# Decoder block on one core: longer first weight pieces and idle products in the opening, compression woven by step length, and the first norm's vectors loaded during the gate

## The chip, the cores and the metric

The kernel runs on one core of a Trainium2 chip. The metric is the device time of one execution in microseconds (us). TensorE is called PE here, VectorE DVE, ScalarE ACT, GpSimd POOL and SyncE SP, as in the profile.

## What is computed

One decoder block for 256 tokens of width 2048, all in float32. Cut to what matters:

```python
proj = x @ w_in
bg, cg, hx, q, k_c, v_c, k_s, v_s, k_w, v_w, ng, ma, mb = _split_in(proj)
y_a = (bg * _causal_dwconv(cg * hx, conv_w)) @ w_conv_out
o_nsa = _nsa(q, k_c, v_c, k_s, v_s, k_w, v_w, sigmoid(ng), pe_k, w1_k, w2_k, pe_v, w1_v, w2_v, rel_bias)
mixed = sigmoid(ma) * y_a + sigmoid(mb) * (o_nsa @ w_attn_out)
x = _layer_norm(DN_ALPHA * x + mixed @ w_mix_out, ln1_g, ln1_b)
h = square(relu(x @ w_mlp_up)) @ w_mlp_down
ple = (p @ w_ple) * sigmoid(x @ w_ple_gate)
x = _layer_norm(DN_ALPHA * x + h + ple, ln2_g, ln2_b)

def _compress(k, pe, w1, w2):      # used by _nsa for keys and for values
    blocks = k[:, idx] + pe        # 15 overlapping windows of 32 tokens, 4 heads
    return gelu(blocks.reshape(..., 32 * 128) @ w1) @ w2
```

## The kernel before

Every weight is read from HBM once, in chunks, by DMAs that SP issues (`load_raw`, L74, four `raw` buffers of 512 KB). A chunk is split into two float32r parts: ACT copies it to the high part `whi` (L82, four buffers), and DVE subtracts that from the chunk to give the low part `wlo` (L84, three buffers). Activations are split in the same way (`split`, L68 on ACT and L69 on DVE). A product is then the sum of three: high by high, high by low and low by high.

`wstat` keeps a weight tile in PE and streams the tokens: for each of 16 k-tiles (128 rows of the weight) and each tile of 128 columns, one 512-column product with `whi` (L100, both parts of the activation) and one 256-column product with `wlo` (L106). It works on 256 weight columns, so on two of the four `mm` buffers of PSUM, and its evacuation (here `add_to`, L185 on ACT and L186 on DVE) frees them. `xstat` keeps the tokens in PE and streams the weights (L127, L128, L131). Both are generators that yield after each chunk.

The opening (L208 to L251) loads x in eight pieces of two k-tiles (L211), turns each with four PE transposes (L179) into a `tp` buffer and splits it into X. The first `wstat`, on the first half of C_KC (256 columns), takes its weights in chunks of two k-tiles (256 KB) and calls `x_ahead`, which loads and turns the next piece of x. Then come a few small things (vectors, a table product `pr` L244, its copy `rv` L246, a store to DRAM `rd` L247 on POOL's queue, from which the first `bias` is read back on ACT's queue, L395, into DVE's copies `cb`, L399 and L400), and the other half of C_KC and the two halves of C_VC in chunks of four k-tiles (512 KB).

The next stage weaves two streams. The main one projects four halves of C_KS and C_KW (`wstat`), C_VS (`xstat` of 512 columns) and C_VW twice (`xstat` of 280 columns). The side one runs `compress` for keys and then for values (L257 to L327): PE turns the position embedding `pn` (L263) to `peT`, DVE adds it to the 32-token windows (L271, four times), ACT and DVE split the sum into `blk` (L68, L69), and PE multiplies `blk` by eight chunks of w1 into `ph` (L281, L282). `weave` gives the side stream 24 turns spread evenly over the 40 steps of the main one, each step counted alike.

Much later, ln1's factor and offset are loaded in broadcast form into `gb` on ACT's queue (L594, L595) behind the mix projection. The first norm, the per-layer embedding, the gate (L653 to L665) and then the MLP follow. The second norm's vectors `gb2` are loaded by L670 and L671.

The order on each engine comes from the tile framework's scheduler, which works from its own estimate of costs; `tc.issue_after(ins)` forces what is written inside it to be issued behind `ins`. Each engine then runs its list in that order and waits on semaphores. A step that waits holds up all that stands behind it on its engine.

Of the kernel before, what the change touches and what calls it, by code (L numbers as in the profile page):

```python
# [45 lines left out]
def block_kernel(ctx: ExitStack, tc: tile.TileContext, x, p, w_in, conv_w, cmp_pe_k, cmp_w1_k, cmp_w2_k,  # L46
# [19 lines left out]

    def split(src, hi, lo):
        nc.scalar.activation(hi, src, AF.Copy)  # L68
        return nc.vector.tensor_sub(lo, src, f32(hi)).ins  # L69

# [6 lines left out]
    def wchunk(src, nk, n, behind=None):  # L77

        raw = load_raw(src, nk, n)
        hi = wp.tile([P, nk, n], F32R, tag="whi", name="whi", bufs=4)  # L80
        lo = wp.tile([P, nk, n], F32R, tag="wlo", name="wlo", bufs=3)
        nc.scalar.activation(hi, raw, AF.Copy)  # L82
        with tc.issue_after(behind) if behind is not None else nullcontext():
            nc.vector.tensor_sub(lo, raw, f32(hi))  # L84
        return hi, lo

    def wstat(src, c0, mov, evac, r0=0, nk=4, ahead=None):


        ps = [ps_mm.tile([P, 2, T], F32, tag="mm", name="mm") for _ in range(2)]  # L90
        for k0 in range(0, KT, nk):
            hi, lo = wchunk(src[r0 + k0 * P:r0 + (k0 + nk) * P, c0:c0 + 256], nk, 256)
            for kk in range(nk):
                kt = k0 + kk
                if ahead is not None:
                    ahead(kt)

                def high():
                    for f in range(2):
                        nc.tensor.matmul(ps[f].rearrange("p a t -> p (a t)"), hi[:, kk, f * P:(f + 1) * P],  # L100
                                         mov[:, kt].rearrange("p a t -> p (a t)"), start=(kt == 0),
                                         stop=(kt == KT - 1), skip_group_check=True)

                def low():
                    for f in range(2):
                        nc.tensor.matmul(ps[f][:, 1, :], lo[:, kk, f * P:(f + 1) * P], mov[:, kt, 0, :],  # L106
                                         start=False, stop=False, skip_group_check=True)
# [4 lines left out]
        for f in range(2):  # L112
# [35 lines left out]
    def weave(main, n_main, side, n_side):  # L148

        done = 0  # L150
        for i, _ in enumerate(main):
            while done * n_main < (i + 1) * n_side:
                next(side, None)
                done += 1
        run(side)
# [16 lines left out]
    def transposed(nat, kt, behind=None):  # L172
# [3 lines left out]
        with tc.issue_after(behind) if behind is not None else nullcontext():  # L176
# [31 lines left out]
    with tc.tile_pool(name="front", bufs=1) as fp:  # L208
        xnat = big.tile([P, NT, D], F32, tag="B", name="xnat")
        def x_load(kt):  # L210
            nc.sync.dma_start(xnat[:, :, kt * P:(kt + 2) * P],  # L211
                              x[:, kt * P:(kt + 2) * P].rearrange("(t p) d -> p t d", p=P))
# [36 lines left out]
        run(wstat(w_in, C_KC + 256, X, add_to(craw[:, 0, 2:4])))  # L249
# [96 lines left out]
        weave(chain(*proj), 40, chain(compress(0, cmp_pe_k, cmp_w1_k, cmp_w2_k),  # L346
# [308 lines left out]

    for j in range(4):
        cs = slice(j * 512, (j + 1) * 512)

        def ev_gate(t, ps):
            sg = post.tile([P, 512], F32, tag="sg", name="sg")  # L660
            nc.scalar.activation(sg, ps, AF.Sigmoid)
# [3 lines left out]
                  behind=(lambda k2: x1_ts[k2]) if j == 0 else None))  # L665

# [126 lines left out]
```

## Time and profile before

| | |
|---|---|
| median of 3 runs | 1856.15 us (1854.9 to 1856.57) |
| the profiled execution | 1856.03 us |
| its span, first to last instruction | 1854.1 us |
| PE busy | 1831.3 us, 99% of the span |
| DVE, ACT busy | 61%, 46% |
| bytes moved | 352.92 MB, 190 GB/s on average |

The profile shows one execution. Its span leaves out some 1.9 us around the first and the last instruction. PE is busy nearly throughout, so the order of its instructions and the few places where it stands idle decide the time. A time is a start in us from the beginning of the span unless said otherwise. Records of products overlap, since PE is pipelined; the chain of waits gives the share of each without the overlap.

### The profile page before, as it was taken

The numbers are of one execution on the slowest core, as the hardware profiler recorded it, in microseconds if no ns is written. First come the engines' busy times: TensorE is split into PE (matmuls) and PEld (weight loads), VectorE is DVE, ScalarE is ACT, GpSimd is POOL, SyncE is SP. The second block draws the span as 40 slices with busy tenths as digits, with TensorE's granted clock in tenths as the row PEclk, the third lists the DMA queues.
The fourth block names the chain that finished last, engine by engine and source line by source line (L and its number), as shares of the span: only waits on it lengthen the run. The fifth ranks groups of instructions, "written<-read, shape, count | busy, mean of one in ns | idle before, by whom it ended". The sixth has DMA issues, their size and how long they took to land.

```text
span 1854.1 us, 24809 instructions
## 1 busy us (share of the span) xinstructions
PE 1831.3 (99%) x9441; PEld 1556.9 (84%) x9441; DVE 1129.0 (61%) x1571; ACT 861.0 (46%) x1181; POOL 16.6 (1%) x25
## 2 busy tenths in 40 slices
PE   8999999999999999999999999999999999999997
PEld 7889888888888888888888788888888888888886
DVE  6676776768677444455555655775565566556664
ACT  5555554455455444444443544543444344434541
POOL 1000000000000000000000000000000000000001
PEclk9999999999999999999999999999999999999999
DMA  8768565555555766666665556655665566556671
GB/s 245 231 200 240 170 174 158 162 170 169 168 161 157 243 194 194 193 187 188 192 230 194 205 194 190 191 186 197 191 188 193 193 193 187 192 189 193 194 248 69
DMA packets 262296, 352.92 MB, mean 190 GB/s; under 512 B 11126, under 2 KB 175318, under 8 KB 261409
## 3 DMA queue, kind: packets, MB, share of 16 engines
q1 hardware_dynamic: 258560, 342.27, 59.8%
q10 hardware_dynamic: 3232, 8.65, 1.4%
q8 instruction: 74, 1.21, 0.3%
q0 software_dynamic: 384, 0.41, 0.1%
q14 instruction: 46, 0.37, 0.1%
HBM read 349.17 MB, written 2.12 MB: 189 GB/s over the span
## 4 chain that ended last, share of the span: by engine, by line
PE 97%; DMA 1%; DVE 1%; ACT 0%; issue 0%; SPq 0%; POOLq 0%; POOL 0%; ACTq 0%; DVEq 0%
PE mm L100 29%; PE mm L131 16%; PE mm L128 16%; PE mm L127 16%; PE mm L106 15%; PE mm L739 1%; PE pss L444 1%; PE po L481 1%; PE tp L466 1%; DMA raw<-in_cmp_w_v_dram 0%; DMA raw<-in_w_ple_gate_dram 0%; PE tp L179 0%; PE po L490 0%; PE po L485 0%; DVE wlo L84 0%; PE pq L407 0%
## 5 line engine op out<-in xcount | busy, mean ns | idle before, releaser
L84 DVE TENSOR_TENSOR wlo<-raw,whi 128x1024 fp32r<-128x1024 f32 (+2 forms) x648 | 778.6, 1205 | 592.6 <-PE mm L131 319.7
L82 ACT ACTIVATE whi<-raw 128x1024 fp32r<-128x1024 f32 (+2 forms) x648 | 676.8, 1046 | 753.9 <-PE mm L128 434.2
L100 PE MATMUL mm<-xT,whi 128*128 128x512 f32 x1280 | 402.7, 398 | 0.0
L100 PE MATMUL mm<-x,whi 128*128 128x512 f32 x1024 | 316.9, 395 | 0.0
L106 PEld LDWEIGHTS mm<-xT,wlo 128*128 128x128 f32 x1280 | 234.9, 189 | 52.2 <-issue 0.2
L106 PE MATMUL mm<-xT,wlo 128*128 128x256 f32 x1280 | 250.6, 280 | 0.0
L106 PEld LDWEIGHTS mm<-x,wlo 128*128 128x128 f32 x1024 | 187.9, 188 | 42.5
L100 PEld LDWEIGHTS mm<-xT,whi 128*128 128x128 f32 x1280 | 200.3, 189 | 4.6 <-issue 0.6
L106 PE MATMUL mm<-x,wlo 128*128 128x256 f32 x1024 | 196.7, 279 | 0.0
L128 PE MATMUL mm<-whi,h 128*128 128x512 f32 x480 | 186.8, 389 | 0.0
L127 PE MATMUL mm<-whi,h 128*128 128x512 f32 x480 | 186.8, 389 | 0.0
L100 PEld LDWEIGHTS mm<-x,whi 128*128 128x128 f32 x1024 | 158.5, 189 | 2.8
L131 PE MATMUL mm<-wlo,h 128*128 128x512 f32 x480 | 148.0, 390 | 0.4 <-DVE wlo L84 0.4
L127 PE MATMUL mm<-whi,xT 128*128 128x512 f32 (+1 forms) x352 | 130.6, 374 | 1.5 <-ACT whi L82 1.4
L128 PE MATMUL mm<-whi,xT 128*128 128x512 f32 (+1 forms) x352 | 130.0, 372 | 0.0
L131 PEld LDWEIGHTS mm<-wlo,h 128*128 128x128 f32 x480 | 90.0, 188 | 19.8 <-DVE wlo L84 1.2
L128 PEld LDWEIGHTS mm<-whi,h 128*128 128x128 f32 x480 | 90.1, 188 | 18.8
L127 PEld LDWEIGHTS mm<-whi,h 128*128 128x128 f32 x480 | 90.1, 188 | 18.7
L131 PE MATMUL mm<-wlo,xT 128*128 128x512 f32 (+1 forms) x352 | 102.8, 373 | 0.0
L127 PEld LDWEIGHTS mm<-whi,xT 128*128 128x128 f32 x352 | 66.1, 188 | 13.2 <-ACT whi L82 1.9
L128 PEld LDWEIGHTS mm<-whi,xT 128*128 128x128 f32 x352 | 66.1, 188 | 11.2
L131 PEld LDWEIGHTS mm<-wlo,xT 128*128 128x128 f32 x352 | 63.9, 188 | 11.2
(216 smaller groups left out, 1773.3 us busy)
## 6 DMA issues: line engine op xcount, KB each, us to landing
raw<-in_w_in_dram SPq DMA_DIRECT2D x228, 512.0 KB, 3.7
raw<-in_w_mlp_up_dram SPq DMA_DIRECT2D x128, 512.0 KB, 3.8
raw<-in_w_mlp_down_dram SPq DMA_DIRECT2D x128, 512.0 KB, 4.0
raw<-in_w_conv_out_dram SPq DMA_DIRECT2D x32, 512.0 KB, 4.1
raw<-in_w_attn_out_dram SPq DMA_DIRECT2D x32, 512.0 KB, 3.6
raw<-in_w_mix_out_dram SPq DMA_DIRECT2D x32, 512.0 KB, 3.9
raw<-in_w_ple_gate_dram SPq DMA_DIRECT2D x32, 512.0 KB, 3.6
raw<-in_w_in_dram SPq DMA_DIRECT2D x16, 280.0 KB, 3.4
```

The source lines that it names most:

```text
L82: nc.scalar.activation(hi, raw, AF.Copy)
L84: nc.vector.tensor_sub(lo, raw, f32(hi))
L100: nc.tensor.matmul(ps[f].rearrange("p a t -> p (a t)"), hi[:, kk, f * P:(f + 1) * P], mov[:, kt].rearrange("p a t -> p (a t)"), start=(kt ...
L106: nc.tensor.matmul(ps[f][:, 1, :], lo[:, kk, f * P:(f + 1) * P], mov[:, kt, 0, :], start=False, stop=False, skip_group_check=True)
L127: nc.tensor.matmul(ps[t], sta[:, kt, 0, ts], hi[:, kk, :], start=(kt == 0), stop=False)
L128: nc.tensor.matmul(ps[t], sta[:, kt, 1, ts], hi[:, kk, :], start=False, stop=False)
L131: last_mm[0] = nc.tensor.matmul(ps[t], sta[:, kt, 0, ts], lo[:, kk, :], start=False, stop=(kt == nkt - 1)).ins
L444: nc.tensor.matmul(ps, q[:, g, a, t * P:(t + 1) * P], kT[:, j, b, :, :w], start=(n == 0), stop=(n == 2))
L466: nc.tensor.transpose(tp[:, b, k, :], s[:, b, k * P:(k + 1) * P], ident)
L481: nc.tensor.matmul(po, vn[:, b, 0, a, vs], pT[:, c, b, 0:2], start=(n == 0 and b == 0), stop=False, skip_group_check=True)
L739: nc.tensor.matmul(ps, h[:, kt, a, ts], w[:, kt, :], start=(kt == 0 and n == 0), stop=(kt == KT - 1 and n == 2))
```

## The change

It does four things.

1. `wchunk` can put `whi` and `wlo` each behind a given instruction, and `wstat` takes the number of 128-column tiles, `nf`.
2. The opening: twelve products of a zeroed tile (128x64, float32, result unused) are put on PE ahead of the first transposes. All 512 columns of C_KC go through one `wstat` with `nf=4`, in chunks of two k-tiles that now hold 512 KB and with all four `mm` buffers; the run for its second half is gone. Pieces of x are loaded one step earlier. The transposes of a piece stand behind the last product written so far. `whi` of a chunk stands behind the high split of the same piece of x, `wlo` behind the low split.
3. `weave` takes a length for each main step: 4 for the 24 steps of 512 KB, 2 for the 16 of 280 columns. The side stream's 24 turns go by length.
4. The loads of ln1's factor and offset move from behind the mix projection to behind the sigmoids of the gate's first and second column block.

```diff
     def split(src, hi, lo):
-        nc.scalar.activation(hi, src, AF.Copy)
+        last_hi[0] = nc.scalar.activation(hi, src, AF.Copy).ins
         return nc.vector.tensor_sub(lo, src, f32(hi)).ins
...
     def wchunk(src, nk, n, behind=None):
...
-        nc.scalar.activation(hi, raw, AF.Copy)
-        with tc.issue_after(behind) if behind is not None else nullcontext():
+        low, high = behind if isinstance(behind, tuple) else (behind, None)
+        with after(high):
+            nc.scalar.activation(hi, raw, AF.Copy)
+        with after(low):
             nc.vector.tensor_sub(lo, raw, f32(hi))
...
-    def wstat(src, c0, mov, evac, r0=0, nk=4, ahead=None):
-        ps = [ps_mm.tile([P, 2, T], F32, tag="mm", name="mm") for _ in range(2)]
+    def wstat(src, c0, mov, evac, r0=0, nk=4, ahead=None, nf=2, behind=None):
+        ps = [ps_mm.tile([P, 2, T], F32, tag="mm", name="mm") for _ in range(nf)]
         for k0 in range(0, KT, nk):
-            hi, lo = wchunk(src[r0 + k0 * P:r0 + (k0 + nk) * P, c0:c0 + 256], nk, 256)
+            hi, lo = wchunk(src[r0 + k0 * P:r0 + (k0 + nk) * P, c0:c0 + nf * P], nk, nf * P,
+                            behind(k0 // nk) if behind is not None else None)
...
     def weave(main, n_main, side, n_side):
-        done = 0
-        for i, _ in enumerate(main):
-            while done * n_main < (i + 1) * n_side:
+        lengths = [1] * n_main if isinstance(n_main, int) else n_main
+        done, at, total = 0, 0, sum(lengths)
+        for step, _ in zip(lengths, main, strict=True):
+            at += step
+            while done * total < at * n_side:
                 next(side, None)
                 done += 1
-        run(side)
+        run(main, side)
...
+        x_split = []
         def x_turn(kt):
-            tp = transposed(xnat, kt)
-            split(tp, X[:, kt:kt + 2, 0, :], X[:, kt:kt + 2, 1, :])
+            tp = transposed(xnat, kt, last_mm[0])
+            low = split(tp, X[:, kt:kt + 2, 0, :], X[:, kt:kt + 2, 1, :])
+            x_split.append((low, last_hi[0]))
         def x_ahead(kt):
-            if kt % 2 == 0 and kt + 2 < KT:
-                x_load(kt + 2)
-                x_turn(kt + 2)
+            if kt == 0:
+                x_load(2)
+            if kt % 2 == 0 and kt + 4 < KT:
+                x_load(kt + 4)
+            if kt % 2 and kt + 1 < KT:
+                x_turn(kt + 1)
...
+        idle = fp.tile([P, P], F32, name="idle")
+        nc.vector.memset(idle, 0.0)
+        for _ in range(12):
+            pw = ps_po.tile([P, 64], F32, tag="po", name="pw")
+            last_mm[0] = nc.tensor.matmul(pw, idle, idle[:, :64], start=True, stop=True).ins
         x_turn(0)
-        run(wstat(w_in, C_KC, X, add_to(craw[:, 0, 0:2]), nk=2, ahead=x_ahead))
+        run(wstat(w_in, C_KC, X, add_to(craw[:, 0]), nk=2, ahead=x_ahead, nf=4,
+                  behind=lambda k: x_split[k]))
...
-        run(wstat(w_in, C_KC + 256, X, add_to(craw[:, 0, 2:4])))
...
-        weave(chain(*proj), 40, chain(compress(0, cmp_pe_k, cmp_w1_k, cmp_w2_k),
+        weave(chain(*proj), [4] * 24 + [2] * 16, chain(compress(0, cmp_pe_k, cmp_w1_k, cmp_w2_k),
...
-    nc.scalar.dma_start(gb[:, 0, :], ln1_g.to_broadcast([P, D]))
-    nc.scalar.dma_start(gb[:, 1, :], ln1_b.to_broadcast([P, D]))
...
+        if j < 2:
+            with tc.issue_after(gated[-1]):
+                nc.scalar.dma_start(gb[:, j, :], (ln1_g, ln1_b)[j].to_broadcast([P, D]))
```

What the scheduler makes of it is seen in the order of the engines. PE in the opening, before (x4 are the transposes of one piece of x, `mm` the products):

```order
L179 MATMUL tp<-ident,xnat 128x128 x12
L100 MATMUL mm<-xT,whi 128x512 x2
L106 MATMUL mm<-xT,wlo 128x256 x2
L100 MATMUL mm<-xT,whi 128x512 x2
L106 MATMUL mm<-xT,wlo 128x256 x2
L100 MATMUL mm<-xT,whi 128x512 x2
L106 MATMUL mm<-xT,wlo 128x256 x2
```

and in the change, where old L179, L100 and L106 are L192, L109 and L116:

```order
L250 MATMUL pw<-idle 128x64 x12
L192 MATMUL tp<-ident,xnat 128x128 x4
L109 MATMUL mm<-xT,whi 128x512 x4
L116 MATMUL mm<-xT,wlo 128x256 x4
L192 MATMUL tp<-ident,xnat 128x128 x4
L109 MATMUL mm<-xT,whi 128x512 x4
L116 MATMUL mm<-xT,wlo 128x256 x4
L109 MATMUL mm<-xT,whi 128x512 x4
L116 MATMUL mm<-xT,wlo 128x256 x4
L192 MATMUL tp<-ident,xnat 128x128 x4
```

Three pieces of x were turned ahead of the first product; now one is, and each further one is turned behind the low products of the even k-tile of the chunk before it. ACT and DVE now alternate strictly: split of a piece of x, split of its weight chunk.

DVE around the end of C_KC, before (L186 evacuates `mm`, L271 adds `peT`, `O_88` holds the raw keys and values):

```order
L84 TENSOR_TENSOR wlo<-raw,whi 128x1024 x2
L186 TENSOR_TENSOR O_88<-O_88,mm 128x256
L265 COPY peT<-tp 128x32
L186 TENSOR_TENSOR O_88<-O_88,mm 128x256
L271 TENSOR_TENSOR O_88<-O_88,peT 128x32x15 x2
L84 TENSOR_TENSOR wlo<-raw,whi 128x1024
L399 COPY cb<-bias 128x4x7
L400 COPY cb<-bias 128x4x15
L84 TENSOR_TENSOR wlo<-raw,whi 128x1024 x3
```

and in the change (old L84, L186, L271, L399, L69 are L92, L199, L296, L424, L72):

```order
L72 TENSOR_TENSOR xT<-tp,xT 128x2x256
L92 TENSOR_TENSOR wlo<-raw,whi 128x1024
L340 MEMSET hx 128x512
L92 TENSOR_TENSOR wlo<-raw,whi 128x1024 x3
L199 TENSOR_TENSOR O_88<-O_88,mm 128x256 x4
L296 TENSOR_TENSOR O_88<-O_88,peT 128x32x15 x4
L424 COPY cb<-bias 128x4x7
L425 COPY cb<-bias 128x4x15
L72 TENSOR_TENSOR blk<-O_88,blk 128x32x60
L92 TENSOR_TENSOR wlo<-raw,whi 128x1024 x4
```

The first `wlo` row here is the last chunk of C_KC. The evacuation of all four buffers now stands behind the first three low parts of C_VC, and the fourth low part of C_VC behind the evacuation, the copies that wait for `bias`, and `blk`.

DVE at the second compression, before:

```order
L265 COPY peT<-tp 128x32
L271 TENSOR_TENSOR O_88<-O_88,peT 128x32x15 x4
L84 TENSOR_TENSOR wlo<-raw,whi 128x1024 x2
L69 TENSOR_TENSOR blk<-O_88,blk 128x32x60
L84 TENSOR_TENSOR wlo<-raw,whi 128x560
```

and in the change:

```order
L290 COPY peT<-tp 128x32
L335 TENSOR_TENSOR kc<-pk,kc 128x4x15
L296 TENSOR_TENSOR O_88<-O_88,peT 128x32x15 x4
L427 CAST kcp<-kc 128x2x4x16
L92 TENSOR_TENSOR wlo<-raw,whi 128x1024
L72 TENSOR_TENSOR blk<-O_88,blk 128x32x60
L92 TENSOR_TENSOR wlo<-raw,whi 128x1024 x8
```

On PE the transpose of `pn` and the first `ph` are now four and a half k-tiles of the 512-column `xstat` apart (a whole k-tile four times, then the high products of one more); before there were six whole k-tiles and the high products of a 280-column one.

## Rows read from the trace of the kernel before

**Rows 1.** The core's span and mean granted clock

```profile
core 0: 1854.1 us, clock 0.998
```

**Rows 2.** Timeline of PE in the opening: start, us, what [idle before <-releaser]

```profile
3.87 1.08 PE L179 MATMUL tp<-ident,xnat 128*128 128x128 f32 x4 [3.87 <-DMA xnat<-in_x_dram]
5.95 1.12 PE L179 MATMUL tp<-ident,xnat 128*128 128x128 f32 x4 [1.00 <-DMA xnat<-in_x_dram]
...
13.00 0.60 PE L179 MATMUL tp<-ident,xnat 128*128 128x128 f32 x4
```

**Rows 3.** Chain of waits, opening and C_VC: start us, us, what

```profile
8.75 0.85 PE mm L100 x2
...
12.46 0.47 PE mm L100 x2
...
35.84 0.93 PE mm L100 x4
...
46.54 0.47 PE mm L106 x4
...
57.70 0.47 PE mm L106 x4
```

**Rows 4.** Timeline of ACT in the opening, columns as in rows 2

```profile
5.42 0.63 ACT L82 ACTIVATE whi<-raw 128x512 fp32r<-128x512 f32 x1 [3.18 <-DMA raw<-in_w_in_dram]
5.96 0.58 ACT L68 ACTIVATE xT<-tp 128x512 fp32r<-128x512 f32 x1
...
13.63 0.60 ACT L68 ACTIVATE xT<-tp 128x512 fp32r<-128x512 f32 x1 [0.20 <-PE tp L179]
...
20.86 1.06 ACT L82 ACTIVATE whi<-raw 128x1024 fp32r<-128x1024 f32 x1 [0.45 <-PE mm L100]
21.84 0.48 ACT L246 ACTIVATE rv<-pr 16x384 f32<-16x384 f32 x1
...
26.89 0.40 ACTq L395 DMA_DIRECT2D bias<-rd  x1
```

**Rows 5.** Timeline of DVE in the opening

```profile
22.43 0.48 DVE L315 MEMSET hx<- 128x512 f32 x1
23.48 2.36 DVE L84 TENSOR_TENSOR wlo<-raw,whi 128x1024 fp32r<-128x1024 f32 x2 [0.57 <-issue]
25.76 0.41 DVE L186 TENSOR_TENSOR O<-O,mm 128x256 f32<-128x256 f32 x1
...
32.91 0.19 DVE L399 COPY cb<-bias 128x28 f32<-128x28 f32 x1 [3.34 <-DMA bias<-rd]
```

**Rows 6.** Timeline of PE around the first compression's end: a float32 product

```profile
123.46 0.55 PE L306 MATMUL pk<-g,w2s 128*128 128x60 f32 x4
123.82 0.48 PE L128 MATMUL mm<-whi,xT 128*128 128x512 f32 x1
```

**Rows 7.** Tile bias: all four reads, us to landing

```profile
DMA to landing us min/median/max: 3.4/4.6/6.0
```

**Rows 8.** Timeline of DVE at the second compression

```profile
126.62 3.75 DVE L271 TENSOR_TENSOR O<-O,peT 128x480 f32<-128x480 f32 x4
...
132.56 2.15 DVE L69 TENSOR_TENSOR blk<-O,blk 128x1920 fp32r<-128x1920 f32 x1
```

**Rows 9.** Timeline of PE at the second compression

```profile
125.16 0.24 PE L263 MATMUL tp<-ident,pn 32*128 32x32 f32 x1
...
134.85 0.35 PE L281 MATMUL ph<-whi,blk 128*120 128x256 f32 x1 [0.56 <-DVE blk L69]
```

**Rows 10.** Stretches: us, busy of PE, PEld, DVE, ACT, POOL, clock, DMA, GB/s

```profile
8.00:12.00 4.00, 4.00 (x15) 3.42 (x14) 2.48 (x5) 1.75 (x3) 0.00 (x0) 1.00 1.09 326
...
148.00:153.00 5.00, 3.64 (x29) 3.42 (x28) 1.97 (x2) 2.23 (x3) 0.00 (x0) 1.00 0.85 266
158.00:163.00 5.00, 4.87 (x38) 4.62 (x37) 3.70 (x6) 2.97 (x6) 0.00 (x0) 1.00 0.66 175
```

**Rows 11.** Stretches after ln1's loads and at the norm, same columns

```profile
945.00:955.00 10.00, 10.00 (x49) 8.29 (x48) 4.73 (x5) 3.59 (x5) 0.00 (x0) 1.00 0.98 374
...
1035.00:1045.00 10.00, 8.35 (x44) 6.54 (x43) 4.97 (x9) 5.59 (x9) 0.00 (x0) 1.00 0.70 273
1045.00:1055.00 10.00, 8.20 (x38) 6.27 (x38) 9.23 (x16) 6.94 (x12) 0.00 (x0) 1.00 0.31 109
```

**Rows 12.** Tile gb: the loads of the second norm's factor

```profile
L670 ACTq DMA_DIRECT2D gb<-in_ln_g_dram x1: 334/334/334, 1031.1 to 1031.1; - x1
```

More of the change, by code (lines that the diff above doesn't have):

```diff
@@ L65, in f32, with after @@
         return ap.bitcast(F32)
+    def after(ins):
+        return tc.issue_after(ins) if ins is not None else nullcontext()
     def split(src, hi, lo):
-        nc.scalar.activation(hi, src, AF.Copy)
+        last_hi[0] = nc.scalar.activation(hi, src, AF.Copy).ins
         return nc.vector.tensor_sub(lo, src, f32(hi)).ins
+    last_hi = [None]
     def load_raw(src, nk, n):
@@ L98, in high @@
                 def high():
[L99 to L102, printed above, removed]
+                    for f in range(nf):
+                        last_mm[0] = nc.tensor.matmul(
+                            ps[f].rearrange("p a t -> p (a t)"), hi[:, kk, f * P:(f + 1) * P],
+                            mov[:, kt].rearrange("p a t -> p (a t)"), start=(kt == 0), stop=(kt == KT - 1),
+                            skip_group_check=True).ins
                 def low():
-                    for f in range(2):
-                        nc.tensor.matmul(ps[f][:, 1, :], lo[:, kk, f * P:(f + 1) * P], mov[:, kt, 0, :],
-                                         start=False, stop=False, skip_group_check=True)
+                    for f in range(nf):
+                        last_mm[0] = nc.tensor.matmul(ps[f][:, 1, :], lo[:, kk, f * P:(f + 1) * P],
+                                                      mov[:, kt, 0, :], start=False, stop=False,
+                                                      skip_group_check=True).ins
                 for part in ((high, low) if kt < KT - 1 else (low, high)):
@@ L111, in wstat @@
             yield
-        for f in range(2):
+        for f in range(nf):
             evac(f, ps[f][:, 0, :], ps[f][:, 1, :])
@@ L175, in transposed @@
         tp = pool.tile([P, 2, T], F32, tag=tag, name="tp")
-        with tc.issue_after(behind) if behind is not None else nullcontext():
+        with after(behind):
             for k in range(2):
@@ L210, in x_load @@
         def x_load(kt):
-            nc.sync.dma_start(xnat[:, :, kt * P:(kt + 2) * P],
-                              x[:, kt * P:(kt + 2) * P].rearrange("(t p) d -> p t d", p=P))
+            return nc.sync.dma_start(xnat[:, :, kt * P:(kt + 2) * P],
+                                     x[:, kt * P:(kt + 2) * P].rearrange("(t p) d -> p t d", p=P)).ins
+        x_split = []
         def x_turn(kt):
-            tp = transposed(xnat, kt)
-            split(tp, X[:, kt:kt + 2, 0, :], X[:, kt:kt + 2, 1, :])
+            tp = transposed(xnat, kt, last_mm[0])
+            low = split(tp, X[:, kt:kt + 2, 0, :], X[:, kt:kt + 2, 1, :])
+            x_split.append((low, last_hi[0]))
         def x_ahead(kt):
-            if kt % 2 == 0 and kt + 2 < KT:
-                x_load(kt + 2)
-                x_turn(kt + 2)
+            if kt == 0:
[4 more added lines that the diff above has]
+                x_turn(kt + 1)
         warm = fp.tile([P, 1], F32, name="warm")
@@ L654, in x1_ahead @@
             x1_turn(kt + 6)
+    gated = []
     for j in range(4):
@@ L660, in ev_gate @@
             sg = post.tile([P, 512], F32, tag="sg", name="sg")
-            nc.scalar.activation(sg, ps, AF.Sigmoid)
+            gated.append(nc.scalar.activation(sg, ps, AF.Sigmoid).ins)
             nc.vector.tensor_mul(ple[:, t, cs], sg, ple[:, t, cs])
```

## Prediction

> **What bounds the kernel now.** I read the core's span first: 1854.1 us at a mean granted clock of 0.998 [rows 1]. The profiled execution took 1856.03 us, 0.12 below the median of 1856.15; the sum is made against 1856.03. PE is busy for 99% of the span, so there is almost nothing to win inside the long stages, and a part of the change counts only where PE starts late or stands idle. Three such places are touched.
>
> The first is the opening. PE waits for x until 3.87 and again at 5.95 [rows 2]. Its first products then run at 0.85 us for two of 512 columns, from 12.46 on at 0.47 [rows 3]. That is the ratio of TensorE's two levels, 1.2 and 2.4 GHz, though the column of the granted clock reads 1.00 in that stretch too [rows 10]. From there PE has no gap to the end of C_KC (35.84 + 0.93 = 36.8) and of C_VC (57.70 + 0.47 + 0.93 = 59.1) [rows 3]. One `wstat` of 64 products takes 57.70 - 46.54 = 11.16 us, a k-tile 0.70 [rows 3]. The second place is the second compression: PE waits 0.56 for `blk` [rows 9] and loses 5 - 3.64 = 1.36 and 5 - 4.87 = 0.13 us later in the weave [rows 10]. The third is the norm, where PE loses 1.65 and 1.80 us in two stretches, while the stretch behind ln1's loads is full [rows 11].
>
> A measurement of this kernel can tell about 0.2%, some 3.7 us, from no change.
>
> **The opening, chunk by chunk.** The products are the same in number. What changes is the chain that feeds them. In the new order the transposes of piece n stand behind the low products of the chunk before, and on ACT and DVE a chunk's split stands behind the split of its piece of x. So from the transposes of one piece to those of the next:
>
> - transposes to the start of the high split of x: 13.63 - 13.00 = 0.63 [rows 2, 4];
> - that split until ACT takes the next instruction: 5.96 - 5.42 = 0.54 between two of this size [rows 4];
> - `whi` of 1024 columns: 1.06 [rows 4];
> - `wlo`, half of 2.36: 1.18 [rows 5];
> - four low products: 0.47 [rows 3], and some 0.12 for three handovers at 0.03 to 0.05 (13.63 against 13.00 + 0.60 in the first item).
>
> That is 4.0 us. PE's own work per chunk is 0.44 for the transposes (an estimate, the 0.60 of [rows 2] less the overlap into the next product) and two k-tiles with 4 products of 0.235 and 0.47 of low ones: 3.25. PE stands idle for some 0.75 us in each of seven chunks. Before, it could work ahead, since three pieces had been turned before the first product, and a chunk's split was not tied to x.
>
> Start: x's first piece (256 KB) and the first chunk (now 512 KB) are 768 KB; before, 768 KB had landed at 5.95 [rows 2]. So `whi` ends at 7.0, `wlo` at 8.2, the second transposes start at about 8.8, those of the eighth piece, called E, at 8.8 + 6 x 4.0 = 32.8. C_KC ends at E + 4.0 + 0.47 + 0.93 = E + 5.4 = 38.2, against 36.8 before: +1.4. (Before, the slow products from 8.75 to 12.46 cost some 1.6 us: 3.7 us that would be 3.7 x 0.47 / 0.85 = 2.1. That loss is gone in this sum, if the first products now run fast; if not, it comes back once, in the first chunk.)
>
> **Idle products.** The nearest row is the two float32 products of 60 columns that take 123.82 - 123.46 = 0.36, so 0.18 each [rows 6]. Twelve of them from about 1.0 us end at 3.2, or at 5.3 at half the clock; the first transposes could not start before 3.87 anyway. The cost is 0, at most 1.4. I take 0, since PE is otherwise empty there.
>
> **The `mm` buffers.** C_KC now holds all four, so C_VC cannot start until DVE has added out the first two. DVE has before that: the last `wlo` (until E + 3.5), the memset `hx` 0.48, three `wlo` of C_VC at 1.18 and two adds of 0.41 [rows 5]: E + 8.4 for the second. PE's first product of the pair can go 0.23 earlier, so C_VC starts at E + 8.2. PE waits 2.8 us where it waited for nothing before.
>
> **The bias chain.** The fourth low part of C_VC now stands on DVE behind the copies that wait for `bias`, and behind `blk`. `rv` starts on ACT behind `whi` of the third chunk, at E + 2.2 + 3 x 1.06 = E + 5.4. From `rv` to the first copy it took 32.91 - 21.84 = 11.1 us (store, `bias` issue at 26.89, landing 6.0) [rows 4, 5]. So the copies come at E + 16.5, then some 0.3 for both, `blk` 2.15 [rows 8] and `wlo` 1.18: E + 20.1. PE gets there after 12 k-tiles and the high products of the thirteenth, E + 8.2 + 12 x 0.70 + 0.46 = E + 17.0. It waits 3.1 us. The four reads of `bias` land after 3.4 to 6.0 [rows 7]; at 3.4 the wait is 0.5. I take 6.0, the same transfer at the same place, and keep 0.5 as the bound.
>
> C_VC then ends at E + 8.2 + 2 x 11.16 + 3.1 = E + 33.6 = 66.4, against 59.1: **+7.3 us**. PE is full behind it, so nothing is made good.
>
> **The weave.** By length, the side stream's second start comes so that only four k-tiles of C_VS and four high products lie between the transpose of `pn` and `ph`: 0.2 + 0.4 for `pk` + 4 x 6 x 0.23 + 0.9 = 7.0 us. The windows' additions started 126.62 - 125.16 = 1.5 after that transpose [rows 8, 9]; with the copy of `kc` ahead of them 1.7. Then 3.75 for the additions, 1.8 for ACT's high half of `blk` (an estimate from its size, 1.06 for 1024 columns) and 2.15 for the low half: 9.4, and 0.1 to PE. PE waits 2.5 us in place of 0.56: +1.9. With 280-column steps and chunks of w1 spread by length, the 1.36 and 0.13 go: net **+0.5**, between -2.1 (no wait at all) and +2.
>
> **ln1's loads.** PE is full behind them [rows 11], so taking them away frees nothing. At the gate they stand on ACT's queue behind a sigmoid that has run, and nothing there waits for them until after the MLP's first products. 0, within 0.5 either way.
>
> **Sum:** 1856.03 + 7.3 + 0.5 = 1863.8 us. The case's own range is 1860 to 1867: 2.6 less if `bias` lands early, 2.6 less from the weave, 1 either way from seven chunks of 0.15, up to 1.4 more from late idle products, and not all of these at once.
>
> **Rivals.**
>
> *Faster: the chain does not bind.* If a chunk's step from transposes to transposes were not above PE's own 3.25 us, as it would be if the splits overlapped more than their rows show, the eighth transposes would start at 8.8 + 6 x 3.25 = 28.3 and C_KC end at 28.3 + 0.44 + 3 x 1.41 = 33.0, 3.8 earlier than before. With DVE no longer behind, the waits at C_VC fall away, and with 1.5 from the weave the time is about 1851. It decides at a step of 3.25 against my 4.0. For it: DVE and ACT have spare time in every chunk. Against: each link is in the order and has a row. 0.13.
>
> *No change: only the chunks cost.* If DVE takes the adds early enough and `bias` is not in the way, what is left is +1.4 from C_KC and +0.5: 1857.9. For it: the copies of `bias` waited 3.34 us before too [rows 5] with no loss on PE. Against: DVE runs its list in order, and three `wlo` stand ahead of the adds. 0.20.
>
> *The ln1 move clears the norm.* If the loads that crowd the norm were ln1's, the 3.45 us of [rows 11] would go: 1863.8 - 3.45 = 1860.4. But the loads there are the second norm's [rows 12], which stay. 0.05, still slower than before by over 0.2%.
>
> *Slower: the clock falls.* PE now has a gap in every chunk. If it ran at the lower of its two levels through the opening, the transposes would take 0.9 (the 1.08 of [rows 2], less the overlap) and the two k-tiles 4 x (0.85 + 0.43) = 5.1: 6.0 a chunk instead of 4.0, 14 us over seven chunks, so about 1878. For it: the products at 8.75 were slow after gaps of 1.00 and 0.57 us. Against: behind the gaps of the weave the clock stayed at 1.00 [rows 10]. 0.05. The Trainium skill, "TensorE: Matmul & The Clock Gate", section "A second HAM failure mode: psum-queue depth-cycling", says that short idle stretches between groups of matmuls can make the clock swing between its levels; no run of this kernel with a gap in each chunk is at hand, so by that rule alone it would be this rival.
>
> **How the numbers follow.** Forecast 0.57, faster 0.13, no change 0.20, the ln1 rival 0.05, the clock 0.05. The first and the last two are slower: 0.67. The range leaves out the clock's case and that of the faster rival, and reaches down over no change: 1855.5 to 1867.5. The time is that of the likeliest case.
>
> **What would show it.** Right: in the opening, idle of PE ahead of old L106 released by `wlo`, about seven times 0.4 and as much ahead of L100 released by `whi`; transposes 4.0 us apart; a wait of about 2.8 ahead of the first C_VC product released by the adds, with some 3 us lost in its first half to a late `wlo` behind the `bias` copies; some 2.5 before the second `ph`, and no loss in the 280-column steps; the stretches from 1035 on like those before, shifted. Wrong: transposes 3.3 us apart, or a C_VC without a gap at its start. A first product later than 8.4 would speak for late idle products.

## The result, and the profile after

The changed kernel takes 1867.26 us (median of 6 runs, 1866.53 to 1868.45) against 1856.36 for the kernel before in the same runs: 10.9 us slower, ratio 1.0061, 95% interval [1.0048, 1.0074]. The direction was right; the forecast of 1863.8 was 3.5 us short. The time lies just under the upper edge of the stated range (1867.5) and just above the 1860 to 1867 that the sum gave by itself.

The profiled execution took 1866.53 us, the fastest of the six. The page of the change:

```profile
span 1864.8 us, 24834 instructions
PE 1842.5 (99%) x9465; PEld 1563.5 (84%) x9465; DVE 1130.2 (61%) x1568; ACT 860.2 (46%) x1177; POOL 16.6 (1%) x25
```

Four times along the program show where the 10.7 us of span come from (the first from the chain of waits, as in [rows 3], the others each the start of a product):

| | before | after | later by |
|---|---|---|---|
| end of C_VC's last product | 59.1 | 73.1 | 14.0 |
| first scores of attention (tile `pss`) | 212.3 | 225.6 | 13.3 |
| last product of old L127 with `mix` (before the norm) | 1028.9 | 1042.2 | 13.3 |
| first product that reads `h` (second half of the MLP) | 1225.3 | 1235.8 | 10.5 |

So the opening lost 14.0 us where the forecast had 7.3, the weave gave 0.7 back, and 2.8 us came back between the norm and the MLP, where the forecast had nothing.

The timeline of PE in the opening of the change (start, us, what, and in brackets the idle time before it and what ended it), to be held against [rows 2, 3]:

```profile
1.06 8.90 PE L250 MATMUL pw<-idle 128*128 128x64 f32 x24 [1.06 <-DVE tab L264]
9.75 1.06 PE L192 MATMUL tp<-ident,xnat 128*128 128x128 f32 x4
12.45 2.07 PE L109 MATMUL mm<-xT,whi 128*128 128x512 f32 x4 [1.63 <-ACT whi L90]
...
15.17 1.06 PE L192 MATMUL tp<-ident,xnat 128*128 128x128 f32 x4
```

The twelve idle products (24 records, two for each float32 product) take 8.90 us, 0.74 each, and the first transposes stand behind them: 9.75 in place of 3.87 [rows 2]. The first real products are as slow as before, 2.07 us for four.

From there the chunks follow at the pace that was worked out. ACT's timeline, the splits of three successive pieces of x:

```profile
20.34 0.60 ACT L71 ACTIVATE xT<-tp 128x512 fp32r<-128x512 f32 x1 [2.53 <-PE tp L192]
...
24.41 0.60 ACT L71 ACTIVATE xT<-tp 128x512 fp32r<-128x512 f32 x1 [2.53 <-PE tp L192]
...
28.48 0.60 ACT L71 ACTIVATE xT<-tp 128x512 fp32r<-128x512 f32 x1 [2.53 <-PE tp L192]
```

They are 4.07 us apart. At C_VC the timeline of PE shows both waits that were forecast, and the table of stretches (busy of PE, PEld, DVE, ACT, POOL, then granted clock, DMA share, GB/s) something that was not:

```profile
47.87 0.80 PE L109 MATMUL mm<-xT,whi 128*128 128x512 f32 x1 [1.94 <-DVE O L199]
...
59.38 0.51 PE L116 MATMUL mm<-xT,wlo 128*128 128x256 f32 x2 [0.42 <-DVE wlo L92]
```

```profile
44.00:45.00 1.00, 1.00 (x10) 1.00 (x9) 1.00 (x2) 1.00 (x2) 0.00 (x0) 1.00 0.33 25
...
48.00:49.00 1.00, 1.00 (x3) 0.90 (x4) 1.00 (x4) 0.42 (x1) 0.00 (x0) 0.50 0.93 313
...
50.00:51.00 1.00, 1.00 (x4) 0.83 (x4) 1.00 (x2) 0.00 (x0) 0.00 (x0) 0.50 1.07 378
51.00:52.00 1.00, 1.00 (x7) 0.88 (x6) 1.00 (x2) 0.00 (x0) 0.00 (x0) 0.85 1.08 320
52.00:53.00 1.00, 1.00 (x8) 0.87 (x7) 0.43 (x1) 0.54 (x1) 0.00 (x0) 1.00 1.08 342
```

PE waits 1.94 us for the adds. Behind that gap the granted clock is 0.50, the level of 1.2 GHz, until about 51.4. Some 3.5 us of work run at half speed, so about 1.7 us are lost. PE then comes so late to the fourth low part that it waits only 0.42 there.

The second compression, to be held against [rows 9]:

```profile
127.75 0.24 PE L288 MATMUL tp<-ident,pn 32*128 32x32 f32 x1
...
137.18 0.35 PE L306 MATMUL ph<-whi,blk 128*120 128x256 f32 x1 [2.15 <-DVE blk L72]
```

From the transpose to `ph` it is 9.4 us, as worked out, with a wait of 2.15 in place of 0.56; the 280-column steps have no gap any more. At the norm, chain of waits before, then chain of waits and timeline of the change:

```profile
1033.97 8.66 DMA raw<-in_w_ple_gate_dram
```

```profile
1047.23 5.82 DMA raw<-in_w_ple_gate_dram
```

```profile
1060.07 0.73 PE L138 MATMUL mm<-whi,x 128*128 128x512 f32 x2 [0.90 <-ACT x L71]
1061.03 0.74 PE L139 MATMUL mm<-whi,x 128*128 128x512 f32 x2 [0.23 <-DVE x L72]
```

The gate's weight chunk that PE waits for lands 5.82 us after its issue, and PE's gaps are short; in the kernel before it took 8.66 us, from 1033.97 on, and [rows 11] show the loss.

### The profile page after: what moved, and what is told of

The parts are those of the page before. It is cut to its first block, busy times and chain, and to the rows that moved or that the text cites. A ratio compares the mean times of both kernels' runs of the same rounds, so it can differ in the third digit from the quotient of the medians.

```text
span 1864.8 us, 24834 instructions
## 1 busy us (share of the span) xinstructions
PE 1842.5 (99%) x9465; PEld 1563.5 (84%) x9465; DVE 1130.2 (61%) x1568; ACT 860.2 (46%) x1177; POOL 16.6 (1%) x25
## 4 chain that ended last, share of the span: by engine, by line
PE 94%; issue 2%; DMA 1%; DVE 1%; ACT 0%; POOL 0%; POOLq 0%; DVEq 0%; ACTq 0%
PE mm L109 28%; PE mm L142 16%; PE mm L139 16%; PE mm L138 16%; PE mm L116 14%; PE mm L765 1%; PE pss L469 1%; PE po L506 1%; PE tp L491 1%; DVE wlo L92 0%; PE ph L306 0%; PE ph L307 0%; PE po L515 0%; PE po L510 0%; DMA raw<-in_w_ple_gate_dram 0%
## 5 line engine op out<-in xcount | busy, mean ns | idle before, releaser
L92 DVE TENSOR_TENSOR wlo<-raw,whi 128x1024 fp32r<-128x1024 f32 (+1 forms) x644 | 779.1, 1212 | 584.4 <-PE mm L142 327.3
L90 ACT ACTIVATE whi<-raw 128x1024 fp32r<-128x1024 f32 (+1 forms) x644 | 676.1, 1052 | 743.9 <-PE mm L139 437.1
L109 PE MATMUL mm<-xT,whi 128*128 128x512 f32 x1280 | 403.8, 400 | 4.3 <-ACT whi L90 2.3
L109 PE MATMUL mm<-x,whi 128*128 128x512 f32 x1024 | 316.8, 395 | 0.0
L116 PEld LDWEIGHTS mm<-xT,wlo 128*128 128x128 f32 x1280 | 232.9, 189 | 53.1 <-DVE wlo L92 3.9
L116 PE MATMUL mm<-xT,wlo 128*128 128x256 f32 x1280 | 250.9, 281 | 0.9 <-DVE wlo L92 0.6
L116 PEld LDWEIGHTS mm<-x,wlo 128*128 128x128 f32 x1024 | 187.9, 188 | 42.5
L109 PEld LDWEIGHTS mm<-xT,whi 128*128 128x128 f32 x1280 | 202.9, 190 | 13.0 <-ACT whi L90 4.2
L116 PE MATMUL mm<-x,wlo 128*128 128x256 f32 x1024 | 196.7, 279 | 0.0
L109 PEld LDWEIGHTS mm<-x,whi 128*128 128x128 f32 x1024 | 158.4, 189 | 2.8
```

The source lines that it names most:

```text
L109: last_mm[0] = nc.tensor.matmul(ps[f].rearrange("p a t -> p (a t)"), hi[:, kk, f * P:(f + 1) * P], mov[:, kt].rearrange("p a t -> p (a t)" ...
L116: last_mm[0] = nc.tensor.matmul(ps[f][:, 1, :], lo[:, kk, f * P:(f + 1) * P], mov[:, kt, 0, :], start=False, stop=False, skip_group_check= ...
```

## Experiments

All ratios are to the kernel before in the same runs, with 95% intervals. Runs of the kernel before range from 1851 to 1861 us, so a term below 2 us is read from traces rather than from times.

### Without idle products, and with idle products that do not wait

```diff
-        for _ in range(12):
-            pw = ps_po.tile([P, 64], F32, tag="po", name="pw")
-            last_mm[0] = nc.tensor.matmul(pw, idle, idle[:, :64], start=True, stop=True).ins
```

> The changed kernel without its twelve idle products and without the memset of their operand. Theory A (the idle products hold back the first transposes: these ran at 9.75 us, 5.9 us after x's first piece had landed in the kernel before): the first transposes run at about 3.9, the first product at about 7, and the time falls by 5 to 6 us against the change, so it stays 5 to 6 us above the kernel before. Rival B (the idle products pay for their time, since without them the first chunks run at the low level of the clock for longer): the transposes come earlier but the second and third chunk take over 5 us instead of 4.5 and 4.07, and the time falls by less than 2 us.

Measured: 1864.02 us, ratio 1.0050 [1.0036, 1.0064]. Timeline of PE:

```profile
4.18 1.09 PE L192 MATMUL tp<-ident,xnat 128*128 128x128 f32 x4 [4.18 <-DMA xnat<-in_x_dram]
6.90 2.07 PE L109 MATMUL mm<-xT,whi 128*128 128x512 f32 x4 [1.63 <-ACT whi L90]
...
14.15 0.60 PE L192 MATMUL tp<-ident,xnat 128*128 128x128 f32 x4
...
18.22 0.60 PE L192 MATMUL tp<-ident,xnat 128*128 128x128 f32 x4
```

The transposes start 5.6 us earlier and the first product at 6.9. The chunks are no slower than with idle products, so rival B falls. C_VC ends at 67.0 instead of 73.1. At attention 4.6 us of this are left (221.0 against 225.6), for here the clock fell behind the wait for `blk` too:

```profile
132.00:134.00 2.00, 2.00 (x11) 2.00 (x11) 0.92 (x2) 1.06 (x1) 0.00 (x0) 0.50 0.31 79
```

Another 1.3 go at the norm in this execution: from the last product of old L127 with `mix` to the first with `h` it takes 194.9 us, against 193.6 in the change's. The time falls by less than expected: the two intervals overlap, and the medians differ by 3.2 us, the ratios by 2.0.

```diff
-        for _ in range(12):
-            pw = ps_po.tile([P, 64], F32, tag="po", name="pw")
+        pw = ps_po.tile([P, 64], F32, tag="po", name="pw")
+        for _ in range(12):
```

> The changed kernel with its twelve idle products written to one tile that is taken once, so that none waits for the one before it. In the change each took 8.90 / 12 = 0.74 us. Theory A (it is the wait of each product for the last, besides the two passes of a float32 product, that makes them slow): at 0.2 to 0.4 us each they end between 3.5 and 6, the transposes start at 3.9 to 6, and the time is 4 to 6 us below the change. Rival B (a float32 product with its weight load takes 0.74 us by itself at the low clock): they end near 9.9 as before, and the time is that of the change within 1 us.

Measured: 1866.11 us, ratio 1.0054 [1.0039, 1.0068]. Timeline of PE:

```profile
1.06 5.38 PE L250 MATMUL pw<-idle 128*128 128x64 f32 x24 [1.06 <-DVE tab L264]
6.23 1.06 PE L192 MATMUL tp<-ident,xnat 128*128 128x128 f32 x4
8.92 2.08 PE L109 MATMUL mm<-xT,whi 128*128 128x512 f32 x4 [1.63 <-ACT whi L90]
...
44.34 0.50 PE L109 MATMUL mm<-xT,whi 128*128 128x512 f32 x1 [1.98 <-DVE O L199]
56.00 0.51 PE L116 MATMUL mm<-xT,wlo 128*128 128x256 f32 x2 [2.01 <-DVE wlo L92]
```

Stretches behind the two gaps:

```profile
46.00:48.00 2.00, 2.00 (x14) 1.72 (x13) 2.00 (x4) 0.00 (x0) 0.00 (x0) 1.00 1.07 356
...
58.00:60.00 2.00, 2.00 (x10) 1.81 (x9) 1.25 (x2) 0.62 (x2) 0.00 (x0) 0.50 1.00 324
```

Without the wait an idle product takes 0.45 us, with it 0.74: the wait for the one before is 0.29 of it. The transposes start 3.5 us earlier, but the time stays within about a microsecond, so neither theory is right about the time. Behind the 1.98 us ahead of C_VC the clock did not fall here; PE came early to the fourth low part and waited 2.01 us for it, and behind that gap the clock fell after all. What the slow clock costs in one place, the bias chain takes in another. The 5.4 us of narrow idle products also left the first real products at 2.08 us for four: for these they bought nothing.

### The clock behind a gap

```diff
+        with tc.issue_after(last_mm[0]):
+            for _ in range(8):
+                last_mm[0] = nc.tensor.matmul(pg, wide[:, :P], wide, start=True, stop=True).ins
         for h in range(2):
             run(wstat(w_in, C_VC + 256 * h, X, ...
```

> The changed kernel with eight wide idle products (128x512, float32r, result unused) put on PE between the last product of C_KC and the first of C_VC, where PE stood idle for 1.94 us and then ran at a granted clock of 0.50 from 48 to 51 us. The scheduler also puts the fourth low part of C_VC ahead of blk here, 2.15 us earlier on DVE. Theory A (the idle stretch made the clock fall): the clock stays at 1.00 behind the gap, two products of 512 columns take 0.47 there, and the first half of C_VC ends 1.5 to 2.5 us earlier; 0 to 3 us below the change. Rival B (the clock falls there for another reason, the load of the chip or the transfers): 0.50 again behind the gap, and the time is that of the change within 1 us.

Measured: 1868.03 us, ratio 1.0070 [1.0055, 1.0084]. Timeline of PE, then stretches:

```profile
45.66 1.98 PE L280 MATMUL pg<-wide 128*128 128x512 f32 x8
47.77 0.50 PE L109 MATMUL mm<-xT,whi 128*128 128x512 f32 x1
...
135.56 0.54 PE L313 MATMUL ph<-whi,blk 128*120 128x256 f32 x1 [2.15 <-DVE blk L72]
```

```profile
48.00:50.00 2.00, 2.00 (x13) 1.72 (x13) 2.00 (x5) 0.25 (x1) 0.00 (x0) 1.00 1.03 364
...
136.00:138.00 2.00, 2.00 (x11) 2.00 (x11) 0.86 (x2) 0.58 (x1) 0.00 (x0) 0.50 0.11 15
138.00:140.00 2.00, 2.00 (x12) 1.83 (x11) 1.69 (x2) 1.38 (x2) 0.00 (x0) 0.80 0.79 260
```

With PE busy through the gap the clock stays at 1.00. That fits an idle stretch as the cause, but it is one execution, and behind the 1.98 us above the clock stayed as well. C_VC ends at 71.5 instead of 73.1; the clock alone did not do this, since the fourth low part stood ahead of `blk` here and PE waited 0.32 for the fifth. The time is not lower: in this execution the clock fell behind the 2.15 us at `blk`, where it had not in the change's, and attention starts at 225.5 against 225.6. Over the kernels read so far and three below (adds ahead, early turns, weave alone), PE stood idle for 1.9 to 2.2 us eleven times in the opening and the weave, the start aside. Behind eight of these gaps the clock fell to 0.50, behind three it did not (the `blk` wait of the change and of the run with the adds ahead, and the 1.98 us above). Behind the idle stretches of each chunk of C_KC it never fell, the granted clock being 1.00 from 20 to 45 us in the change. At the norm, with one to three gaps of 0.8 to 1.9 us, it fell in some executions and not in others (neither in the kernel before nor in the change).

### The adds ahead, and the pieces of x turned earlier

```diff
+        added = last_add[0]
         for h in range(2):
-            run(wstat(w_in, C_VC + 256 * h, X, add_to(craw[:, 1, 2 * h:2 * h + 2])))
+            run(wstat(w_in, C_VC + 256 * h, X, add_to(craw[:, 1, 2 * h:2 * h + 2]),
+                      behind=(lambda k: added if k else None) if h == 0 else None))
```

> The changed kernel without idle products, and with the low parts of C_VC's second and later chunks of its first half behind the adds that free C_KC's four mm buffers. In the run without idle products PE waited 1.95 us ahead of C_VC for these adds and then ran at half the clock. Theory A (the wait is DVE's order, three low parts ahead of the adds): PE waits 0.7 to 1.2 us there, the clock does not fall behind so short a gap, and the time is 1 to 3 us below the run without idle products. Rival B (the wait is for ACT's copies or for the last product, not for DVE's order): the wait stays near 1.9 us and the time stays.

Measured: 1860.54 us, ratio 1.0024 [1.0013, 1.0035], so 0.26% or 4.8 us below the run without idle products by the ratios. Timeline of PE:

```profile
41.32 0.50 PE L109 MATMUL mm<-xT,whi 128*128 128x512 f32 x1 [0.39 <-DVE O L199]
```

The wait is 0.39 us, the clock stays at 1.00 behind it, and C_VC ends at 64.4 in place of 67.0 though the first product of the opening came 0.5 us later. The scheduler also put the fourth low part of C_VC ahead of the copies of `bias` on DVE, and PE no longer waits for it. It was DVE's order. The gain is more than the 1 to 3 us expected: the end of C_VC shows 2.6 of it, and in this execution the clock did not fall behind the wait for `blk`, where it fell in the run without idle products.

```diff
             if kt == 0:
                 x_load(2)
+                x_turn(2)
...
-            if kt % 2 and kt + 1 < KT:
-                x_turn(kt + 1)
+            if kt % 2 and kt + 3 < KT:
+                x_turn(kt + 3)
```

> The run with the adds ahead (no idle products), and each piece of x turned one chunk earlier: the transposes of piece n now stand behind the low products of the chunk two before, not of the one before. Theory A (the chain from the transposes through both splits to the low products sets the pace of a chunk, 4.07 us in the change against 3.25 of PE's own work): chunks follow each other at 3.2 to 3.4 us, PE has no gap in C_KC, and the time is 4.5 to 6 us below the run with the adds ahead, so about that of the kernel before. Rival B (the pace is set by ACT, DVE or the transfers themselves): chunks stay at 3.8 us or more and the time falls by less than 2 us.

Measured: 1855.61 us, ratio 0.9999 [0.9991, 1.0007], the time of before. Timeline of PE, transposes of three successive pieces:

```profile
14.71 0.60 PE L192 MATMUL tp<-ident,xnat 128*128 128x128 f32 x4
...
17.92 0.60 PE L192 MATMUL tp<-ident,xnat 128*128 128x128 f32 x4
...
21.16 0.60 PE L192 MATMUL tp<-ident,xnat 128*128 128x128 f32 x4
```

They are 3.2 us apart, PE's own work, in place of 4.07, and no gap is left in C_KC. ACT, DVE and the transfers keep up with that, so the pace was set by the chain alone. Its worth is 4.6 us by the ratios (1.0024 to 0.9999) and 3.7 by the end of C_VC (60.6 against 64.4); the profiled execution, at 1858.34 us, is the slowest of its twelve.

### The weave alone

```diff
-        weave(chain(*proj), 40, ...
+        weave(chain(*proj), [4] * 24 + [2] * 16, ...
```

> The kernel before with the weave by lengths alone. Theory A: PE waits some 2.2 us for blk at the second compression in place of 0.56, and the losses of 1.36 and 0.13 in the 280-column steps are gone; the net is between -0.6 and +0.5 us. Rival B (the 280-column steps were worth more than was seen): 1.5 us or more below before.

Measured: 1857.87 us, ratio 1.0011 [1.0002, 1.0019]: 2 us slower. The interval, 0.4 to 3.5 us, reaches down to the upper end of theory A, and rival B falls. Timeline of PE and stretches:

```profile
122.90 0.35 PE L283 MATMUL ph<-whi,blk 128*120 128x256 f32 x1 [2.15 <-DVE blk L69]
```

```profile
124.00:126.00 2.00, 2.00 (x11) 1.91 (x10) 1.49 (x2) 1.53 (x2) 0.00 (x0) 0.53 0.38 99
```

The wait of 2.15 us and the end of the other gaps are as expected; what was left out is the clock behind the wait, again some 1.7 us. Attention starts 0.6 later than before in this trace (212.9 against 212.3); where the rest of the 2 us lies is not shown.

### The norm

```diff
-    nc.scalar.dma_start(gb[:, 0, :], ln1_g.to_broadcast([P, D]))
-    nc.scalar.dma_start(gb[:, 1, :], ln1_b.to_broadcast([P, D]))
...
+        if j < 2:
+            with tc.issue_after(gated[-1]):
+                nc.scalar.dma_start(gb[:, j, :], (ln1_g, ln1_b)[j].to_broadcast([P, D]))
```

> The kernel before with the move of ln1's two loads alone. Behind the weave the change was 13.3 us late, at the end only 10.7: it made good 2.6 us at the norm, where the chunk of the gate's weight landed in 5.82 us instead of 8.66. Theory A (the prediction's: the loads at the norm are the second norm's, so the move frees nothing, and the 2.6 us are a matter of when these transfers meet): the same as before within 1 us. Rival B (the move makes the norm's transfers faster): 2 to 3 us below before, and the gate's first weight chunk lands in about 6 us.

Measured: 1855.01 us, ratio 0.9997 [0.9989, 1.0006]: the same. Chain of waits:

```profile
1034.94 8.54 DMA raw<-in_w_ple_gate_dram
```

The gate's chunk takes 8.54 us with ln1's loads gone as well. So the move is worth nothing, as forecast, and the change's 5.82 us have another cause. The next run tried the number of transfers.

```diff
-        run(wstat(w_in, C_KC, X, add_to(craw[:, 0, 0:2]), nk=2, ahead=x_ahead))
+        run(wstat(w_in, C_KC, X, add_to(craw[:, 0, 0:2]), nk=4, ahead=x_ahead))
```

> The kernel before with the first half of C_KC in four chunks of 512 KB instead of eight of 256 KB, so with as many weight transfers as the change. In the three runs with the new opening the second norm's vectors land 4.9 and 7.1 us after their issue, in the three with the old one 7.6 to 7.7 and 10.3 to 10.4. Theory A (the number of transfers ahead of them decides how these meet at the norm): they land at 4.9 and 7.1 here too, and PE loses 2 to 3 us less at the norm. Rival B (it is something else in the new opening): 7.7 and 10.4. The opening itself may end up to 2 us later, since the first product has to wait for 512 KB.

Measured: 1858.23 us, ratio 1.0013 [1.0004, 1.0022]. Tile `gb`, the second norm's vectors:

```profile
DMA to landing us min/median/max: 7.7/9.1/10.4
```

Rival B: 7.7 and 10.4. Of the 2 us, 0.4 are there at the end of C_VC (59.5 against 59.1) and 1.7 where attention starts (214.0 against 212.3), so most are lost in the weave. Nor is it the new opening. The run with the filled gap has that opening and 7.7 and 10.3; the run with wide idle products below has the old one and 4.9 and 7.2. What decides between the two in an execution stays open. What it costs was tested by taking these loads away:

```diff
+        if j > 1:
+            with tc.issue_after(gated[-1]):
+                nc.scalar.dma_start(gb2[:, j - 2, :], (ln2_g, ln2_b)[j - 2].to_broadcast([P, D]))
...
-    nc.scalar.dma_start(gb2[:, 0, :], ln2_g.to_broadcast([P, D]))
-    nc.scalar.dma_start(gb2[:, 1, :], ln2_b.to_broadcast([P, D]))
```

> The kernel before with the second norm's two loads moved behind the sigmoids of the gate's third and fourth column block; ln1's loads stay. In ten profiled executions these loads landed after 4.9 and 7.1 us in four, after 7.6 to 7.8 and 10.3 to 10.4 in five and in between in one, whatever the kernel. Theory A (their 2 MB share the transfer of the gate's first weight chunk, and the lost time at the norm is this): the gate's chunk lands in under 5 us, PE loses less than 1.5 us at the norm instead of 3.45, and the time is 2 to 4 us below before. Rival B (PE waits at the norm for the splits of the normed x, not for the weight): the same as before within 1 us.

Measured: 1852.77 us, ratio 0.9985 [0.9976, 0.9994], 2.8 us below before. Timeline of PE at the norm, its only gap there:

```profile
1048.14 0.74 PE L128 MATMUL mm<-whi,x 128*128 128x512 f32 x2 [1.34 <-DVE x L69]
```

No DMA is left in the chain at the norm. From the last product of L127 with `mix` to the MLP's first with `h` it is 193.5 us (1029.4 to 1222.9) against 196.4 before (1028.9 to 1225.3). It was the second norm's loads, not the first's, that stood in the way of the gate's weights. (ACT, which waited 3.03 us for that chunk before, does not wait for it here.)

### Putting together what helped

```diff
+        pw = ps_po.tile([P, 512], F32, tag="po", name="pw")
+        for _ in range(6):
+            pwi = nc.tensor.matmul(pw, wide[:, :P], wide, start=True, stop=True).ins
-        x_turn(0)
+        x_turn(0, pwi)
```

> The kernel before with six wide idle products (128x512, float32r) ahead of the first transposes, in place of the change's twelve narrow ones of float32, which ended late and left the first real products as slow as before. Theory A (PE busy with wide products before x lands brings the full clock earlier): the products at 8.4 us take less than 0.85 for two, the opening ends 0.5 to 1.6 us earlier, and the time is that much below before. Rival B (the gaps of 1.00 and 0.57 us between the first transposes undo it, or the products do not count): the first products are as slow as before, and the time is the same.

Measured: 1855.81 us, ratio 1.0006 [0.9995, 1.0016]: no difference. Timeline of PE:

```profile
1.46 2.93 PE L230 MATMUL pw<-wide 128*128 128x512 f32 x6 [1.46 <-DVE tab L243]
...
8.61 0.73 PE L100 MATMUL mm<-xT,whi 128*128 128x512 f32 x2 [0.36 <-DVE xT L69]
```

In the kernel before:

```profile
8.40 1.20 PE L100 MATMUL mm<-xT,whi 128*128 128x512 f32 x2
```

Behind six wide products in 2.93 us PE comes to full speed earlier: the first two pieces of x are turned as slowly as before (1.05 and 1.11), the third in 0.63 in place of 1.11, and the first two products take 0.73 in place of 1.20. That it is the width that counts is not shown, since this opening also has other gaps (0.33, 0.94 and 0.36 us) than the one with narrow products (1.63). Attention starts 1.0 us earlier (211.3). In this execution the clock fell to 0.50 behind the gaps at the norm, 0.77 and 1.22 us, and the microsecond is not seen in the time.

> The kernel before with both edits that looked good one by one: six wide idle products ahead of the first transposes, and the second norm's loads behind the gate. If the two add up, 3 to 5 us below before (1 from the opening, 2 to 4 from the norm); if the norm's loads are not what PE waits for, 0 to 1 below.

Its edits are those of the two runs before. Measured: 1856.49 us, ratio 1.0004 [0.9995, 1.0012]: they do not add up. Attention starts at 211.1, but at the norm PE waits 1.93 us for DVE's split of the normed x, where it waited 1.34 with the loads moved alone, and the clock falls behind it:

```profile
1047.43 0.85 PE L128 MATMUL mm<-whi,x 128*128 128x512 f32 x2 [1.93 <-DVE x L69]
```

```profile
1049.00:1051.00 2.00, 2.00 (x6) 1.60 (x5) 1.94 (x3) 0.75 (x2) 0.00 (x0) 0.50 0.56 210
```

From `mix` to `h` it is 196.1 us, about as long as before. Why the split comes later here stays open.

The last run is the change without idle products, with the adds ahead, the early turns, the weave as before, and both norms' loads during the gate.

> All that helped, on the changed kernel: no idle products, the adds ahead, each piece turned one chunk earlier, the weave by steps counted alike as before, ln1's loads during the gate's first two column blocks and the second norm's during its last two. If the parts add up: the run with early turns (the time of before), less 1 to 2 us for the wait of 2.15 us at the second blk, less 3 us at the norm: 3 to 5 us below before, at or below the run with the second norm's loads moved alone (3.2 below). Rival: the scheduler orders the norm otherwise with all of these together, and the time is within 1.5 us of before.

Measured: 1855.07 us, ratio 0.9989 [0.9980, 0.9998]: 1.7 us below before. The parts do not add up fully here either. The stretch from `mix` to `h` has its gain (193.6 us), but attention starts at 213.6, 1.3 later than before. By its ratio the move of the second norm's loads alone is the best version found, though the two intervals overlap.

## Why the prediction was right or wrong

**The step that failed is the price of the idle products.** It read "the cost is 0, at most 1.4", from two float32 products at 0.18 us each [rows 6], doubled for the lower clock. They took 0.74 each: 0.45 by themselves and 0.29 for the wait of each on the one before, which comes from the single `po` buffer and stands in the program. They held back the first transposes to 9.75, by 5.6 us. Without them C_VC ends at 67.0, where the sum had 66.4; with them at 73.1.

**The chunk chain was right.** Forecast 4.0 us, measured 4.07, and 3.2 with early turns against 3.25 for PE's own work. It is worth 3.7 us at the end of C_VC, 4.6 by the ratios.

**The buffers and the bias chain were right in place and too large in size.** Forecast 2.8 and 3.1 us, measured 1.94 and 0.42 in the change. Between them lies what the sum left out, 1.7 us of slow clock behind the first wait, and with a fast clock there the second wait was 2.01. From the eighth transposes to the end of C_VC it is 73.1 - 40.2 = 32.9 us against 33.6 forecast: that the sum is nearly right here is in part luck, since the slow clock it left out stands in for the waits that it had too large.

**The first products stayed slow.** The sum let them run fast, with 1.6 us to come back if not. They did come back, as some 1.8: from transposes to transposes the first chunk took 5.4 us and the second 4.5, in place of 4.07 each.

**The clock rival was put in the wrong place.** It was to fall through the short gaps of every chunk, at 0.05. It did not fall there, but behind gaps of 2 us. With the rule of the Trainium skill, "TensorE: Matmul & The Clock Gate", section "A second HAM failure mode: psum-queue depth-cycling", that short idle stretches between groups of matmuls can make the clock swing, the traces agree for gaps of 1.9 to 2.2 us, with 0.50 behind eight of eleven; the stretches of under a microsecond in each chunk do not show it.

**The weave:** +0.5 forecast, -0.7 in the profiled execution of the change and +2 in the time of the weave alone. The wait of 2.15 had been put at 2.5; the sign hangs on the clock behind it.

**ln1's loads:** nothing forecast, nothing measured. The 2.8 us that the change made good at the norm come from how the second norm's loads happened to land in that execution, and they hid part of the loss: with the loads late and the clock falling at the norm too, as in the run with the filled gap, the span was 1868.7 against 1864.8. So it is in part luck that the forecast came as near as 3.5 us.

The rival of a faster time needed the chunk chain not to bind, and the rival of an unchanged time needed the adds and `bias` not to hold up PE. The chain did bind, at 4.07 us a chunk, and the waits came, 1.94 and 0.42 us.

At the end of C_VC the traces divide the 14.0 us: 6.1 for the idle products (73.1 to 67.0), 2.6 for the adds' order with the slow clock behind the wait (to 64.4), 3.7 for the chunk chain (to 60.6), and 1.5 that are left against 59.1 and that no run took apart. By the ratios the loss is 2.0 us for the idle products (1.0061 to 1.0050), 4.8 for the adds' order with the slow clock behind the wait (to 1.0024) and 4.6 for the chunk chain (to 0.9999); the first is the least certain, since its trace still shows 4.6 at attention.

## What to carry to other kernels

An order forced between two streams makes a chain of every link it ties, so add the links up and hold them against the busiest engine's own work per round; one round of slack (here turning x one chunk earlier) took the whole chain away. Price a filler by its own form: small float32 products that wait for each other in one buffer cost four times what a distant row of fast ones suggested, and the first real products behind them were as slow as without them. When loads crowd a stage, look up which loads they are before moving any.

## What the runs showed of the hardware

- Behind a gap of 1.9 to 2.2 us on PE the granted clock fell to 0.50 in eight of eleven cases and some 3.4 us of work then ran at half speed, about 1.7 us each time; whether it falls varies from one execution to the next at the same place. Behind the 0.39 us gap and those in each chunk it stayed at 1.00, and behind the norm's shorter gaps both are seen.
- At the start of the program products run at about half speed while the column of the granted clock reads 1.00: four wide ones took 2.07 us in the first chunk and 1.20 later. Behind 5.4 us of narrow idle products (128x64, float32) they still took 2.08; behind 2.9 us of wide ones (128x512, float32r), in the opening of the kernel before, two took 0.73 in place of 1.20.
- Two broadcast loads of 1 MB on ACT's queue landed after 4.9 and 7.1 us in four profiled executions, after 7.6 to 7.7 and 10.3 to 10.4 in five and in between in two, and no edit tried decides which. Where the clock stayed at 1.00 at the norm, the stretch from `mix` to `h` took 193.6 to 194.9 us in the first group and 196.4 to 196.5 in the second.
